# A fused gated convolution, pooling and MLP block on eight cores: staging the output projection's norm chain, issuing MLP weight loads as buffers come free, reordering the first loads and pacing the pooling

## The chip, the cores and the metric

The kernel runs on all 8 cores of one Trainium2 chip. Each core computes 2048 of the 16384 positions by itself; the cores exchange nothing. The metric is device time in microseconds (us) of the slowest core. Some executions fall into a slower state, in which the cores of one die (cores 0 to 3 or 4 to 7) show a lower granted clock (the share of TensorE's full clock that it was allowed, 1.00 at most) and the time is some per cent longer, whatever the kernel. The experiments were made in four groups, each on one chip together with the kernel before, and the chips differ a little: the fast runs of the kernel before lie between 1048.4 and 1053.2 us.

## The reference

```python
u = rms_norm(x, mix_pre_g)
proj = u @ w_in                                   # columns: GLU 2x1024, pooling 1024, gates 2x1024
y_conv = conv_branch(proj[GLU])                   # GLU, depthwise conv 31, layer norm, swish, @ w_conv_out
y_pool = pool_branch(proj[pool])                  # trailing means (2,4,8,16) minus token, per-group linear, @ w_pool_out
merged = sigmoid(g_conv) * y_conv + sigmoid(g_pool) * y_pool
h = x + rms_norm(merged @ w_o, mix_post_g)        # "output projection"
v = rms_norm(h, mlp_pre_g)
v = square(relu(v @ w_ff1)) @ w_ff2               # "FF1", "FF2", hidden width 4096
out = h + rms_norm(v, mlp_post_g)
```

Inputs and outputs are float32, shape (4, 4096, 1024). The kernel multiplies in bf16.

## The kernel before

Every operation goes through a helper that records what it reads and writes and adds the waits, so the order of the calls in Python is the order in which each engine works. That is why most lines of the profile carry the line of a helper: L220 is a matmul, L223 a transpose on TensorE, L238 an ACTIVATE on ScalarE, L241 and L250 are VectorE operations, L262 a weight load issued by POOL that casts float32 to bf16. A load or store on SP's queue is `LOAD` or a plain `dma_start`.

The first loads and the front, in which a tile `x_norm(j)` is normalised, `x_tr(j)` transposes it, and `p_group` multiplies it with the pooling columns of `w_in`:

```python
x_order = [0, 1, 2, 3, -1] + list(range(4, 16))   # -1 is the halo tile of 32 rows
x_load(0); LOAD(grow, gbd[0:1, :]); x_load(1); LOAD(identf, identd); x_load(2); x_load(3); LOAD(vec[:], vecs)
for i in range(2):                                # pooling weights in two pieces
    WLOAD(w_p[:, :, i * 512:(i + 1) * 512], ...)
# ...
for cc in range(4): p_group(cc, 0, 256)
x_tr(2); x_norm(-1); x_tr(3); x_norm(4)
wg_load(0); wg_load(1)                            # 4 MB of GLU weights
for cc in range(4): p_group(cc, 256, 256)
x_tr(-1); x_norm(5)
for cc in range(4, 8):
    p_group(cc, 0, 512)
    if cc == 5 or cc == 6:
        x_tr(cc - 1); x_norm(cc + 1)
p_halo()
for j in (6, 7): x_tr(j); x_norm(j + 2)
# blocks 1 to 3 follow
```

The output projection of a tile of 128 positions, with its two norms in one row of calls:

```python
def resid(b, gb_t, epsc, res, junk, j, eng):
    for hh in range(2): ACT(junk, ps[:, b + hh, :], AF.Square, accum=...)      # sums, ScalarE
    TTE("dve", ...)                                                            # add the halves
    rsqrt(r, ac[0], epsc, eng)                                                 # two operations on POOL
    for hh in range(2):                                                        # scale, add x, VectorE
        STT(ps[:, b + hh, :], ps[:, b + hh, :], r, gb_t[...], ALU.mult, ALU.mult)
        TTE("dve", rs, ps[:, b + hh, :], rs, ALU.add)
    outh[j] = ... dma_start(out=out[128 * j:128 * (j + 1), :], in_=res)        # store h

def wo_tile(j):
    b = banks(2)                                     # 16 matmuls into two PSUM banks
    # ...
    res, dst = xr[j % 3], xb2[j % 2]
    resid(b, gb1, 2, res, dst[:, 0:512], j, "pool")
    r = rstd(res, 128, 0, dst, "pool")               # second norm: ScalarE, then POOL
    STT(dst, res, r, gb2, ALU.mult, ALU.mult)        # VectorE
    if j + 3 < 16: x_reload(j + 3)
```

The four tiles of the last block run between groups of FF1 (block 0), and the weight loads go out of one queue `wq`, one per step:

```python
pend.extend(range(4 * blk, 4 * blk + 4))
for c in (blk, blk + 4): wq.append(lambda c=c: ff1_load(c))
if blk == 3:
    for i in (2, 3, 0, 1): wq.append(lambda i=i: ff2_load(i))
# ...
for i in range(32):
    ff1_group(i, blk)                                # matmuls, relu on VectorE, square on ScalarE
    if blk == 0 and i < 16:
        if i % 4 == 3: wo_step()                     # one wo_tile, one load
        elif i % 4 == 1 and len(trq) > 1: h_tr(trq.popleft())
        if i == 15:
            for s in (4, 5, 6, 7): wq.append(lambda s=s: ff2_load(s))
    if blk == 0 and i >= 16 and wq: wq.popleft()()
```

The FF2 weights lie in eight slots. Slots 4 and 5 hold the residual buffers `xr[0..2]` and a norm gain until the last tile (15) is done, slots 6 and 7 the output weights. FF2 reads the slots in the order 0, 4, 1, 5, 2, 6, 3, 7.

The pooling tasks (VectorE, one for each of 8 channel groups and 4 blocks) are queued and poured out in the first GLU quarter:

```python
for q in range(4):
    for rp in range(8):
        glu_pair(q, rp)
        pump(3)                                      # three pooling tasks
    if q == 0: pump(len(bgd))
```

Of the kernel before, what the change touches and what calls it, by code (L numbers as in the profile page):

```python
# [10 lines left out]
ALU = mybir.AluOpType  # L11
# [159 lines left out]
def build_program():  # L171
# [20 lines left out]
    with ExitStack() as es:  # L192
# [150 lines left out]
        def x_load(j):  # L343
            i = x_order.index(j)
            P, r0 = (32, 0) if j < 0 else (128, H + 128 * j)
            xev[j] = LOAD(xst[i % 4][:P, :], xh[r0:r0 + P, :])

        x_order = [0, 1, 2, 3, -1] + list(range(4, 16))
        x_load(0)
        LOAD(grow, gbd[0:1, :])  # L350
        x_load(1)
        LOAD(identf, identd)
        x_load(2)
        x_load(3)
        LOAD(vec[:], vecs)
        for i in range(2):
            WLOAD(w_p[:, :, i * 512:(i + 1) * 512], w_in_v[:, :, 2048 + i * 512:2048 + (i + 1) * 512])
        for i in range(3):
# [50 lines left out]

        bgd = deque()  # L410

        def pump(n):
# [3 lines left out]

        s2i = {"i": 0}

# [65 lines left out]
        def wg_load(q):  # L484
            for h2 in range(2):
                WLOAD(wg[q % 2][:, :, h2, :], w_in_v[:, :, h2 * 1024 + q * 256:h2 * 1024 + (q + 1) * 256])

        for cc in range(4):
            p_group(cc, 0, 256)
        x_tr(2)  # L490
        x_norm(-1)
        x_tr(3)
        x_norm(4)
        wg_load(0)
        wg_load(1)
        for cc in range(4):
            p_group(cc, 256, 256)
        x_tr(-1)
        x_norm(5)
        for cc in range(4, 8):  # L500
            p_group(cc, 0, 512)
            if cc == 5 or cc == 6:
                x_tr(cc - 1)
                x_norm(cc + 1)
        p_halo()
        for cc in range(8):
            bgd.append(lambda cc=cc: pool_task(cc, 0))
        for j in (6, 7):
            x_tr(j)
            x_norm(j + 2)  # L510
        for blk in range(1, 4):
            for cc in range(8):
                nxt = 4 * (blk + 1) + cc // 2
                if cc % 2 == 0 and nxt + 2 < 16:
                    x_norm(nxt + 2)
                p_group(cc, blk * 512, 512)
                bgd.append(lambda cc=cc, blk=blk: pool_task(cc, blk))
                if cc % 2 == 1 and nxt < 16:
                    x_tr(nxt)
                if cc % 2 == 1 or blk == 3:  # L520
                    pump(1)

# [100 lines left out]
        for q in range(4):  # L623
            glu_halo(q)
            steps = deque(conv_steps(q - 1) if q else [])
            for rp in range(8):
                glu_pair(q, rp)
                pump(3)
                if rp % 2 == 1 and steps:
                    steps.popleft()()  # L630
                if q == 3 and rp % 2 == 0:
                    weff_group(rp // 2)
            if q + 2 < 4:
                wg_load(q + 2)
            if q == 0:
                pump(len(bgd))
            if q == 1:
                weff_prep()
            if q == 2:
                weff_scale()  # L640
                WLOAD(wgp, w_in_v[:, :, 4096:5120])
            if q == 2:
                for r in range(16):
                    bgd.append(lambda r=r: ln_stat(0, r))
# [75 lines left out]

        def resid(b, gb_t, epsc, res, junk, j, eng):
            ac = []
            for hh in range(2):
                a, r = col()
                ACT(junk, ps[:, b + hh, :], AF.Square, scale=1.0 / 32, accum=a)
                ac.append(a)
            TTE("dve", ac[0], ac[0], ac[1], ALU.add)
            r = col()[1]
            rsqrt(r, ac[0], epsc, eng)
            for hh in range(2):  # L730
                rs = res[:, hh * 512:(hh + 1) * 512]
                STT(ps[:, b + hh, :], ps[:, b + hh, :], r, gb_t[:, hh * 512:(hh + 1) * 512], ALU.mult, ALU.mult)
                TTE("dve", rs, ps[:, b + hh, :], rs, ALU.add)
            outh[j] = kb.op("sp", lambda e: e.dma_start(out=out[128 * j:128 * (j + 1), :], in_=res), [res], [("outh", j)], dma=True)

        def x_reload(j):
            LOAD(xr[j % 3], xh[H + 128 * j:H + 128 * (j + 1), :])

        def wo_tile(j):
            b = banks(2)  # L740
            for hh in range(2):
                for k in range(8):
                    MM(ps[:, b + hh, :], m1(j // 4, k)[:, (j % 4) * 128:(j % 4 + 1) * 128], wo[:, k, hh * 512:(hh + 1) * 512], k == 0, k == 7)
            res, dst = xr[j % 3], xb2[j % 2]
            resid(b, gb1, 2, res, dst[:, 0:512], j, "pool")
            r = rstd(res, 128, 0, dst, "pool")
            STT(dst, res, r, gb2, ALU.mult, ALU.mult)
            if j + 3 < 16:
                x_reload(j + 3)

# [16 lines left out]

        def wo_step():

            if pend:  # L770
                j = pend.popleft()
                wo_tile(j)
                trq.append(j)
            if wq:
                wq.popleft()()

        trq = deque()
        wq = deque()
        for blk in range(4):
            for cc in range(8):  # L780
                gated(cc, blk, wco, s_t, wgc, False)
                if blk and cc % 2 == 1:
                    wo_step()
                elif blk and len(trq) > 1:
                    h_tr(trq.popleft())
            pend.extend(range(4 * blk, 4 * blk + 4))
            for c in (blk, blk + 4):
                wq.append(lambda c=c: ff1_load(c))
            if blk == 0:
                wq.popleft()()  # L790
                wq.popleft()()
            if blk == 3:
                for i in (2, 3, 0, 1):
                    wq.append(lambda i=i: ff2_load(i))

# [9 lines left out]
        def ff2_tile(j):  # L805
# [4 lines left out]
            for hh in range(2):  # L810
                for i in range(32):
                    f = FF1_ORDER[i // 4] * 4 + i % 4
                    MM(ps[:, b + hh, :], h1(i)[:, tl * 128:(tl + 1) * 128], ff2(f)[:, hh * 512:(hh + 1) * 512], i == 0, i == 31)
            resid(b, gb3, 0, res, hT[j // 4][:, 0, :], j, "act")

        for blk in range(4):
            for i in range(32):
                ff1_group(i, blk)
                if blk == 0 and i < 16:
                    if i % 4 == 3:  # L820
                        wo_step()
                    elif i % 4 == 1 and len(trq) > 1:
                        h_tr(trq.popleft())
                    if i == 15:
                        for s in (4, 5, 6, 7):
                            wq.append(lambda s=s: ff2_load(s))
                if blk == 0 and i >= 16 and wq:
                    wq.popleft()()
                if blk == 0 and i >= 18 and trq:
                    h_tr(trq.popleft())  # L830
                if blk == 0 and i == 20:
                    LOAD(gb3, gbd[3:4, :].partition_broadcast(128))
            for tl in range(4):
# [77 lines left out]
```

## Time and profile before

| | kernel before |
|---|---|
| fast runs | 1049.79, 1050.14, 1050.25 us |
| slow run | 1194.67 us |
| profiled core (3) | 1048.2 us |
| TensorE busy | 977.5 us |
| idle at 0 to 88 us (front) | 25.7 us |
| idle at 550 to 660 us (FF1, start of FF2) | 30.5 us |

The two idle figures are 88 or 110 us less the busy time of TensorE in the stretches that the prediction shows. The page's first part, busy time of each engine (share of the span) and number of instructions:

```profile
PE 977.5 (93%) x5172; PEld 491.0 (47%) x5172; DVE 424.4 (40%) x688; ACT 312.3 (30%) x570; POOL 60.9 (6%) x110
```

No engine but TensorE is half busy, so time can only be won where TensorE waits. Lines of a timeline give start, length, engine, line, operation, output and input, shapes, the number of instructions in the row and, in brackets, how long the engine had been idle and what ended it.

### The profile page before, as it was taken

The numbers are of one execution on the slowest core, as the hardware profiler recorded it, in microseconds if no ns is written. First come the engines' busy times: TensorE is split into PE (matmuls) and PEld (weight loads), VectorE is DVE, ScalarE is ACT, GpSimd is POOL, SyncE is SP. The second block draws the span as 40 slices with busy tenths as digits, with TensorE's granted clock in tenths as the row PEclk, the third lists the DMA queues.
The fourth block names the chain that finished last, engine by engine and source line by source line (L and its number), as shares of the span: only waits on it lengthen the run. The fifth ranks groups of instructions, "written<-read, shape, count | busy, mean of one in ns | idle before, by whom it ended". The sixth has DMA issues, their size and how long they took to land.

```text
span 1048.2 us, 14416 instructions; the slowest of 8 cores (1043.8 to 1048.2 us)
## 1 busy us (share of the span) xinstructions
PE 977.5 (93%) x5172; PEld 491.0 (47%) x5172; DVE 424.4 (40%) x688; ACT 312.3 (30%) x570; POOL 60.9 (6%) x110
## 2 busy tenths in 40 slices
PE   3799989999999999999998784999999999999996
PEld 2544647766544544444443331444444444444443
DVE  3377843254363123565665440124412342244222
ACT  3663122333213441334333440113311232123211
POOL 2000001000010000112111120000000000000000
PEclk9999989999999999999999998899999999999999
DMA  9925255996990022628484799121001100220021
GB/s 210 200 83 93 50 82 91 146 169 113 163 150 1 1 81 23 138 82 160 115 178 103 129 173 167 42 81 41 1 31 66 65 1 1 81 81 1 1 81 61
DMA packets 47527, 92.53 MB, mean 88 GB/s; under 512 B 6593, under 2 KB 27329, under 8 KB 46306
## 3 DMA queue, kind: packets, MB, share of 16 engines
q0 software_dynamic: 30336, 46.14, 30.5%
q1 hardware_dynamic: 17122, 45.47, 13.2%
q8 instruction: 43, 0.70, 0.3%
q14 instruction: 26, 0.21, 0.1%
HBM read 120.90 MB, written 16.84 MB: 131 GB/s over the span
## 4 chain that ended last, share of the span: by engine, by line
PE 85%; DMA 6%; DVE 4%; issue 2%; ACT 2%; POOL 1%; DVEq 0%; ACTq 0%; POOLq 0%
PE ps L220 82%; DMA arena<-w_ff 4%; PE ps L223 2%; ACT arena L238 2%; DMA arena<-w_in 2%; DVE arena L241 1%; DVE arena L444 1%; DVE ps L246 1%; DVE arena L250 1%; DVE ps L250 0%; POOL arena L262 0%; POOL sm L378 0%; DVEq L159 0%; ACT sm L238 0%; POOL sm L377 0%
## 5 line engine op out<-in xcount | busy, mean ns | idle before, releaser
L220 PE MATMUL ps<-arena 128*128 128x512 bf16 (+4 forms) x4644 | 951.6, 366 | 52.9 <-DMA arena<-w_ff 16.4
L220 PEld LDWEIGHTS ps<-arena 128*128 128x128 bf16 (+2 forms) x4644 | 458.3, 104 | 526.0 <-issue 79.8
L238 ACT ACTIVATE arena<-ps 128x512 bf16<-128x512 f32 (+5 forms) x386 | 237.2, 634 | 624.9 <-PE ps L220 461.1
L246 DVE TENSOR_SCALAR ps<-ps 128x512 f32<-128x512 f32 x128 | 87.3, 697 | 99.9 <-PE ps L220 99.9
L241 DVE TENSOR_TENSOR arena<-ps,arena 128x512 f32<-128x512 f32 (+3 forms) x116 | 86.8, 754 | 88.8 <-ACT arena L238 58.9
L241 DVE TENSOR_TENSOR sm<-sm 128x1 f32<-128x1 f32 x32 | 5.0, 157 | 208.1 <-ACT arena L238 208.1
L250 DVE SCALAR_TENSOR_TENSOR arena<-arena,ps 128x512 bf16<-128x512 f32 (+1 forms) x64 | 43.8, 684 | 99.3 <-ACT arena L238 71.2
L238 ACT ACTIVATE arena<-arena 128x1024 bf16<-128x1024 f32 (+1 forms) x33 | 34.8, 1053 | 91.7 <-DVE arena L241 87.1
L250 DVE SCALAR_TENSOR_TENSOR arena<-arena,sm 128x1024 bf16<-128x1024 f32 (+1 forms) x33 | 42.4, 1284 | 44.0 <-POOL sm L378 41.8
L250 DVE SCALAR_TENSOR_TENSOR ps<-ps,sm,arena 128x512 f32<-128x512 f32 x64 | 48.2, 754 | 21.3 <-POOL sm L378 19.7
L223 PE MATMUL ps<-identb,arena 128*128 128x128 bf16 (+1 forms) x520 | 37.8, 222 | 9.8 <-DVE arena L250 6.3
L223 PEld LDWEIGHTS ps<-identb,arena 128*128 128x128 bf16 (+1 forms) x520 | 33.4, 100 | 21.8 <-issue 12.4
L241 DVE TENSOR_TENSOR arena<-arena 128x512 bf16<-128x512 f32 (+2 forms) x56 | 38.2, 690 | 4.2
L238 ACT ACTIVATE arena<-ps,vec 128x1024 bf16<-128x1024 bf16 x16 | 19.3, 1205 | 2.5 <-PE ps L223 1.7
L586 DVE BATCH_NORM_STATS2 bnst<-arena 128x6 f32<-128x512 bf16 x32 | 20.0, 680 | 0.0
L262 POOL DMA_DIRECT2D arena<-w_ff x16 | 13.7, 863 | 102.2 <-PE ps L220 101.5
L382 DVE RECIPROCAL sm<-sm 128x1 f32<-128x1 f32 (+1 forms) x33 | 5.3, 161 | 35.1 <-ACT sm L238 35.1
L378 POOL TENSOR_TENSOR sm<-sm,mhalf 128x1 f32<-128x1 f32 x32 | 18.1, 567 | 5.0 <-POOL sm L377 0.4
L250 DVE SCALAR_TENSOR_TENSOR arena<-arena 128x512 bf16<-128x512 f32 x24 | 16.5, 687 | 1.6 <-DVE arena L241 0.5
L262 POOL DMA_DIRECT2D arena<-convw x8 | 4.3, 544 | 208.8 <-PE ps L220 136.1
L377 POOL TENSOR_SCALAR sm<-sm 128x1 f32<-128x1 f32 x32 | 7.0, 220 | 155.4 <-DVE sm L241 80.5
L444 DVE TENSOR_TENSOR_SCAN arena<-arena,scr 128x512 f32<-128x512 f32 x12 | 15.4, 1280 | 0.7
(33 smaller groups left out, 82.9 us busy)
## 6 DMA issues: line engine op xcount, KB each, us to landing
arena<-xh SPq DMA_DIRECT2D x32, 512.0 KB, 6.8
arena<-w_ff POOLq DMA_DIRECT2D x16, 1024.0 KB, 16.1
out<-arena SPq DMA_DIRECT2D x32, 512.0 KB, 2.9
arena<-convw POOLq DMA_DIRECT2D x8, 1536.0 KB, 15.4
arena<-out SPq DMA_DIRECT2D x16, 512.0 KB, 4.2
arena<-w_in POOLq DMA_DIRECT2D x8, 512.0 KB, 25.5
arena<-w_in POOLq DMA_DIRECT2D x2, 2048.0 KB, 24.2
arena<-w_in POOLq DMA_DIRECT2D x2, 1024.0 KB, 24.4
```

Of the source, the lines that this page charges most:

```text
L220: kb.op("pe", lambda e: e.matmul(o, lhsT=l, rhs=r, start=start, stop=stop), [l, r], [o])
L223: kb.op("pe", lambda e: e.transpose(o, i, idn), [i, idn], [o])
L238: kb.op("act", lambda e: e.activation(out=o, in_=i, func=func, **kw), rd, wr)
L241: kb.op(eng, lambda e: e.tensor_tensor(out=o, in0=a, in1=b, op=op), [a, b], [o])
L246: kb.op("dve", lambda e: e.tensor_scalar(out=o, in0=a, scalar1=s1, scalar2=s2, op0=op0, **kw), rd, [o])
L250: kb.op("dve", lambda e: e.scalar_tensor_tensor(out=o, in0=a, scalar=s, in1=b, op0=op0, op1=op1), rd, [o])
L262: return kb.op("pool", lambda e: e.dma_start(out=o, in_=src), [], [o], dma=True, after=after)
L377: kb.op("pool", lambda e: e.tensor_scalar(out=o, in0=i, scalar1=EPS[epsc], scalar2=None, op0=ALU.add), [i], [o])
L378: kb.op("pool", lambda e: e.tensor_tensor(out=o, in0=o, in1=mhalf[:, 0:n], op=ALU.pow), [o, mhalf[:, 0:n]], [o])
L382: kb.op("dve", lambda e: e.reciprocal(o, o), [o], [o])
L444: kb.op("dve", lambda e: e.tensor_tensor_scan(so, pc[:, lo:lo + n], pc[:, lo - w:lo - w + n], init, ALU.add, ALU.subtract), rd, [so])
L586: kb.op("dve", lambda e: e.bn_stats(o, i), [i], [o])
```

## The change

Its intent is to take away four waits of TensorE. Pooling tasks come one per GLU pair, over two quarters, in the order in which later buffers overwrite their inputs. The norm chain is cut into stages one slot (two groups) apart, so that VectorE does not stand and wait for ScalarE and POOL inside it. Weight loads of the MLP go out as soon as their buffers are free. And the first loads go out in the order in which they are wanted, in smaller pieces, with the GLU weights moved out of the front.

```diff
-        x_load(0)
-        LOAD(grow, gbd[0:1, :])
-        x_load(1)
+        LOAD(grow, gbd[0:1, :])
+        x_load(0)
         LOAD(identf, identd)
-        x_load(2)
-        x_load(3)
-        LOAD(vec[:], vecs)
-        for i in range(2):
-            WLOAD(w_p[:, :, i * 512:(i + 1) * 512], ...)
+        for j in (1, 2, 3):
+            x_load(j)
+        for i in range(4):                      # x_load(4) waits for the second of these
+            wev.append(WLOAD(w_p[:, :, i * 256:(i + 1) * 256], ...))
 ... (cut)
-        for cc in range(4):
+        for cc in range(2):
             p_group(cc, 0, 256)
         x_tr(2)
         x_norm(-1)
         x_tr(3)
-        x_norm(4)
-        wg_load(0)
-        wg_load(1)
-        for cc in range(4):
+        LOAD(vec[:], vecs)
+        for cc in range(2):
             p_group(cc, 256, 256)
-        x_tr(-1)
-        x_norm(5)
-        for cc in range(4, 8):
+        for cc in range(2, 8):
             p_group(cc, 0, 512)
-            if cc == 5 or cc == 6:
-                x_tr(cc - 1)
-                x_norm(cc + 1)
+            if cc == 3:
+                x_tr(-1)
+                x_norm(4)
+                x_norm(5)
         p_halo()
-        for j in (6, 7):
+        for j in (4, 5, 6, 7):
             x_tr(j)
             x_norm(j + 2)
 ... (cut: wg_load moved into block 1)
                 glu_pair(q, rp)
+                pool_pump(1)
                 pump(3)
-            if q == 0:
-                pump(len(bgd))
             if q == 1:
+                pool_pump(32)
 ... (cut: resid split into resid_a, the sums and the root, and resid_b, the scaling and the store)
+            r = resid_a(b, 2, dst[:, 0:512], "pool")
+            def stage_b():
+                resid_b(b, gb1, r, res, j)
+                v["r"] = rstd(res, 128, 0, dst, "pool")
+            def stage_c():
+                STT(dst, res, v["r"], gb2, ALU.mult, ALU.mult)
+                if j + 3 < 16:
+                    x_reload(j + 3)
+            due.append(deque([stage_b, stage_c, lambda: h_tr(j)]))
+        def tick():                             # one stage of every tile under way
+            for d in list(due):
+                d.popleft()()
 ... (cut)
             pend.extend(range(4 * blk, 4 * blk + 4))
-            for c in (blk, blk + 4):
-                wq.append(lambda c=c: ff1_load(c))
 ... (cut)
+            ff1_load(blk)
+            ff1_load(blk + 4)
+        for i in (2, 3, 0, 1):
+            ff2_load(i)
 ... (cut)
+                if blk == 0 and i % 2 == 1:
+                    tick()
+                    if i % 4 == 3 and pend:
+                        wo_tile(pend.popleft())
+                    if i == 19:
+                        for n in (4, 5, 6, 7):
+                            ff2_load(n)
```

## The prediction

> **What bounds the kernel now.** I read the engine shares first, then busy time by stage, then what the TensorE waits for, then the timeline inside each hole.
>
> ```profile
> PE   3799989999999999999998784999999999999996
> PEclk9999989999999999999999998899999999999999
> ```
>
> Two strips of the page (busy tenths of TensorE, granted clock) in 40 slices of 26.2 us. TensorE is full but for the front and slices 22 to 26. Busy time in stretches, first number after the length being TensorE's:
>
> ```profile
> 0.00:30.00 30.00, 12.96 (x68) 8.00 (x68) 8.11 (x21) 11.02 (x21) 5.62 (x10) 1.00 0.98 205
> 30.00:88.00 58.00, 49.35 (x362) 27.35 (x363) 38.43 (x72) 36.52 (x71) 0.56 (x1) 0.94 0.69 140
> 88.00:148.00 60.00, 55.23 (x250) 31.16 (x249) 45.43 (x67) 12.33 (x21) 2.30 (x3) 0.94 0.42 59
> 440.00:550.00 110.00, 109.51 (x562) 50.69 (x561) 67.40 (x100) 42.78 (x89) 19.57 (x44) 1.00 0.59 134
> 550.00:610.00 60.00, 45.88 (x235) 21.39 (x234) 30.11 (x45) 23.69 (x49) 13.53 (x26) 0.98 0.61 125
> 610.00:660.00 50.00, 33.59 (x131) 13.55 (x130) 8.58 (x13) 10.46 (x18) 1.54 (x3) 0.84 0.95 154
> ```
>
> Idle: 17.0, 8.7, 4.8, 0.5, 14.1, 16.4 us. From 148 to 550 and from 660 on TensorE has no hole worth naming; the last 7.8 us are the tail. The table of waits names the releasers:
>
> ```profile
> PE ps L220 <- DMA arena<-w_ff: 16.4, 4, 6.8
> PE ps L220 <- ACT arena L238: 14.7, 8, 2.9
> PE ps L220 <- DMA arena<-w_in: 6.9, 1, 6.9
> PE ps L220 <- DVE arena L241: 4.8, 1, 4.8
> ```
>
> The 14 us at 550 to 610, one tile of the output projection on the timeline (start, length, engine, idle before):
>
> ```profile
> 573.25 0.76 DVE L250 SCALAR_TENSOR_TENSOR ps<-ps,sm,arena 128x512 f32<-128x512 f32 x1 [1.21 <-POOL sm L378]
> ...
> 578.95 1.28 DVE L250 SCALAR_TENSOR_TENSOR arena<-arena,sm 128x1024 bf16<-128x1024 f32 x1 [2.62 <-POOL sm L378]
> 580.15 2.48 DVE L246 TENSOR_SCALAR ps<-ps 128x512 f32<-128x512 f32 x4
> 580.93 3.58 ACT L238 ACTIVATE arena<-ps 128x512 bf16<-128x512 f32 x6 [3.25 <-DVE ps L246]
> 581.67 3.61 PE L220 MATMUL ps<-arena 128*128 128x512 bf16 x16 [2.63 <-ACT arena L238]
> ```
>
> VectorE stands 1.21 and 2.62 us inside the norm chain waiting for POOL's reciprocal root; four finished FF1 groups wait behind it, no PSUM bank comes free, TensorE stops 2.63 us. The weights hole:
>
> ```profile
> 605.93 2.32 POOL L262 DMA_DIRECT2D arena<-w_ff  x3
> 608.57 2.97 POOL L262 DMA_DIRECT2D arena<-w_ff  x4 [0.32 <-DVE ps L246]
> ...
> 638.42 3.48 PE L220 MATMUL ps<-arena 128*128 128x512 bf16 x8 [6.84 <-DMA arena<-w_ff]
> 644.64 3.16 PE L220 MATMUL ps<-arena 128*128 128x512 bf16 x8 [2.74 <-DMA arena<-w_ff]
> 650.35 1.89 PE L220 MATMUL ps<-arena 128*128 128x512 bf16 x8 [2.55 <-DMA arena<-w_ff]
> 656.53 13.72 PE L220 MATMUL ps<-arena 128*128 128x512 bf16 x50 [4.29 <-DMA arena<-w_ff]
> ```
>
> Seven FF2 weight loads are issued together at 606 to 611 and land one after another, the last four 6.2, 5.7 and 6.2 us apart (mean 6.0). After a hole eight matmuls take 3.48 us where 1.73 is warm (216 ns each, from 16 in 3.46 elsewhere).
>
> **What the Trainium skill says.** (1) "PSUM — Partial Sum Buffer", section "Engine vs sequencer instructions": "ScalarE/VectorE/GpSimdE queues are strict FIFO". The trace agrees: the four evictions at 580.15 start only when the chain's last operation ends. (2) "TensorE: Matmul & The Clock Gate", section "Back-to-back issue gap": N/1.2 ns cold and N/2.4 + 2.5 ns warm, so 427 and 216 at 512 columns; the trace has 435 (3.48/8) after the 6.84 us hole and 216. Holes thus cost more than their length. (3) "DMA: Bandwidth & Descriptors", section "Issuing engines are not separate DMA queues": transfers from all issuers interleave on the same 16 engines. The trace agrees: in 0 to 22 us POOL's queue has 47.6% and SP's 45.7% of the engines.
>
> **The change, part by part.** Matmul work stays the same; only waits can go.
>
> *Pooling paced.* Before, 16 pooling tasks are poured out in the first GLU quarter, three per pair; after, one per pair over two quarters, in the order in which the next buffers overwrite them. A scan task is 1.28 + 0.15 + 0.69 = 2.1 us of VectorE, a pair needs 0.69 more: 2.8 us beside 3.45 us of matmuls (16 x 216 ns), so it keeps up. The second quarter adds the convolution's four evictions of 1.22: 8 x 2.8 + 4.9 = 27 us in about 36. The hole of 4.77 us at 137.9 goes, and with it its cold start (32 matmuls in 9.75 us where 6.9 is warm, 2.85). Gain 7.6 us.
>
> *Norm chain in stages.* After, the sums, then the scaling and residual, then the second norm, then the transposes are issued one slot (two FF1 groups, 3.45 us) apart. The root needs two POOL operations, 0.22 + 0.57, plus hand-over, 1.2 us seen, so it is ready when its reader's turn comes. VectorE has per tile (four FF1 groups) 4 x 0.70 + 0.16 + 2 x (0.75 + 0.69) + 1.28 = 7.1 us in 10.8 us of TensorE (4 x 1.73 + 3.45 + 0.45). The five holes 0.79, 2.93, 2.63, 2.64, 5.14 go: 14.1, plus cold matmuls and transposes after the last (22.85 for 100 where 21.6, and 1.01 where 0.61): 1.7. I leave 0.5 for imperfection: gain 15.3 us.
>
> *FF loads.* FF1 loads and FF2 loads 2, 3, 0, 1 go out at block ends, the last six at about 539 in today's times: 6 x 6.0 = 36 us, all down by 578, long before use. FF2 4 to 7 lie over the residual buffers and the output weights; they stay bound to the last tile's third stage. FF1 begins at 542.2 (counted back from the timeline); 32 groups 55.3, four tiles 13.8, six transposes 2.7 bring FF2's start to 614.0 instead of 630.7. Group 17 ends at 542.2 + 31.1 + 13.8 + 2.3 = 589.3; scaling 0.9 + 2.9, square 1.3, POOL 0.9, final operation 1.3 end at 596.6. Loads issued there land at about 605, 611, 617, 623 (two to start, 6.0 each). FF2 wants slot 4 at 614.9, 5 at 616.6, 6 at 618.3, 7 at 620.1: only slot 7 is late, 3 us, and costs 2 us of cold clock. Before: 16.4 us of waits and cold excess 1.75 + 1.43 + 0.16 + 2.9 = 6.2, sum 22.7. Gain 22.7 - 5 = 17.7 us.
>
> *First loads.* Norm gains and identity come ahead of x1; pooling weights come in four pieces (the first needs half the bytes); 4 MB of GLU weights leave the front. Before, the first projection starts at 21.85, while the transposed x1 was there at 18.3. After, the first piece should be there at 12 (half of 21.5 less the start), so the x chain decides: identity no longer holds the first transpose (cast at 10.6), about 16. Then what is left in: the copy of x3's transpose still stands behind the halo tile's norm on VectorE, so the 4.46 us hole stays; and now all four transposes of x4 to x7 come after the halo, each with its norm (square 1.55, scaling 1.28, copy 1.0 or 0.7 in a row over two engines). I count 7.7 us from halo to block 1, of which 1.8 transposes, against 3.3 before (48.45 to 51.76). Adding up: 16 + 3 + 5.5 + 2.7 + 3.5 + 0.3 + 6.9 + 1.7 + 7.5 = 47.1 against 51.76. Gain 4.7 us, of the 10 that the earlier start suggests.
>
> Sum: 7.6 + 15.3 + 17.7 + 4.7 = 45.3; 1050.25 - 45.3 = 1005 us.
>
> **Rivals.** (a) *The staging makes a PSUM wait.* A tile holds its two banks a slot longer, and in the gated stage the next tile comes to the same pair: its first bank is free 3.8 us after the even group ends (tanh 0.6, two operations 1.4, scaling and add 1.45, hand-overs), wanted at 3.9. It just fits; if late by 1 us, twelve tiles cost 12 us: 1017. For it: that near tie. Against it: banks are released one by one, and that stage has 0.5 us of idle now. (b) *The late FF2 loads stay the bound.* If the third stage slips or four loads share with other traffic, 10 us of wait instead of 3: 1013. (c) *The front gives it all back* (x4's load now waits for the second weight piece): 1010; or it gives 10: 1000. (d) *Denser matmuls pull the granted clock down.* Full stretches show 1.00 now, so I give it little: 2% of the rest would be 1025.
>
> **Range and chances.** Taking (a), (b) or (c) at part strength: 997 to 1017. Two per cent is 21 us; pooling and chain alone give 23, each read from a hole with a known cause. Faster 0.96, same 0.035, slower 0.005.
>
> **What would show it.** Right: no hole at 130 to 138 (in times moved forward); waits on ScalarE near zero during FF1; TensorE's wait on FF weights 2 to 5 us, once; first projection near 16 us and block 1 near 47. Wrong: a wait on VectorE before each tile in the gated stage (a), several waits on FF weights (b), block 1 at 51 or later (c), or matmuls slower than 216 ns in full stretches (d).

## The result, and the profile after

The kernel after ran at 1020.25, 1019.89 and 1021.38 us in fast runs; two runs were slow (1100.13 and 1120.79, with one die at a clock near 0.89). A ratio here is the mean time of one kernel's fast runs over that of the other's of the same rounds, so it is not quite the ratio of the medians quoted. It is 0.9719, with a 95% interval of 0.9696 to 0.9741: faster, by about 30 us. The prediction said 1005 us, with 997 to 1017: the direction is right, and the time lies above the range.

The same two strips of the page as in the prediction, of the kernel after, in 40 slices of 25.5 us:

```profile
PE   4799999999999999999999996999999999999996
PEclk9799999999999999999999997999999999999999
```

Counting slices from 1, the holes of slices 22 to 24 of before are gone and slice 6 is full; one hole is left, in slice 25, at 611 to 636 us, and the front looks much as it did. Busy time in stretches (TensorE's is the first number after the length; the clock stands before the last two numbers):

```profile
0.00:30.00 30.00, 14.76 (x70) 9.16 (x71) 10.22 (x24) 11.94 (x23) 3.88 (x8) 0.91 1.03 196
30.00:88.00 58.00, 49.69 (x346) 25.61 (x344) 30.13 (x50) 34.99 (x67) 4.08 (x5) 0.90 0.73 149
88.00:148.00 60.00, 60.00 (x289) 36.03 (x288) 43.09 (x72) 15.52 (x25) 2.30 (x3) 1.00 0.40 54
...
440.00:550.00 110.00, 108.76 (x554) 50.23 (x552) 68.08 (x101) 45.36 (x93) 24.25 (x50) 1.00 0.66 140
550.00:610.00 60.00, 59.51 (x307) 27.99 (x305) 34.37 (x50) 28.32 (x53) 8.59 (x18) 1.00 1.05 192
610.00:660.00 50.00, 41.09 (x165) 16.94 (x164) 6.26 (x12) 5.43 (x14) 0.00 (x0) 0.86 0.45 94
```

From 88 to 148 TensorE idles 0.0 us instead of 4.8, from 550 to 610 0.5 instead of 14.1. From 610 to 660 it still idles 8.9 us, and the last but one number of the row above says where to look: the DMA engines were full (1.05) in the stretch before. What TensorE waited for:

```profile
PE ps L223 <- DVE arena L250: 10.7, 5, 3.5
PE ps L220 <- DMA arena<-w_ff: 8.9, 3, 3.7
PE ps L220 <- DVE arena L256: 6.3, 2, 4.3
PE ps L220 <- ACT arena L238: 5.4, 4, 1.4
```

ScalarE's 14.7 us became 5.4, of which 4.2 lie before 88 us (three holes of 1.4) and none in FF1. The waits for FF weights fell from 16.4 us in four holes to 8.9 in three. New at the top are 10.7 us of transposes waiting for a normalised tile (L223 for L250) and 6.3 us of projections waiting for a copy (L256): both are the front. This is the timeline of the hole that is left:

```profile
591.19 20.02 PE L220 MATMUL ps<-arena 128*128 128x512 bf16 x92
614.91 3.31 PE L220 MATMUL ps<-arena 128*128 128x512 bf16 x8 [3.71 <-DMA arena<-w_ff]
621.36 2.93 PE L220 MATMUL ps<-arena 128*128 128x512 bf16 x8 [3.14 <-DMA arena<-w_ff]
626.36 24.01 PE L220 MATMUL ps<-arena 128*128 128x512 bf16 x97 [2.07 <-DMA arena<-w_ff]
```

POOL issues the loads. The first row is the six early ones, the second the last four:

```profile
539.82 4.82 POOL L262 DMA_DIRECT2D arena<-w_ff  x6
...
596.54 3.07 POOL L262 DMA_DIRECT2D arena<-w_ff  x4 [7.39 <-DMA out<-arena]
```

POOL stood 7.39 us before the last four, until a store of `out` had read the residual buffer of tile 15. When each load landed is in the trace too:

```
six early loads, issued 539.8 to 543.9, landed  554.7  564.4  572.3  581.9  589.8  600.7
last four loads, issued 596.5 to 598.8, landed  608.4  614.8  621.2  626.2
store of tile 15, issued 586.8, landed 595.8
```

The prediction had the six "all down by 578"; the sixth landed at 600.7. Transfers of the kernel after from 539.8 to 600.8, the time of the six loads, by queue (packets, MB, share of the 16 DMA engines) and by kind (size in KB written, median us from issue to landing):

```profile
q0 software_dynamic: 4282, 6.48, 77.2%
q1 hardware_dynamic: 1428, 5.22, 25.7%
...
arena<-w_ff POOLq DMA_DIRECT2D x10, 1024.0 KB, 25.5
out<-arena SPq DMA_DIRECT2D x5, 512.0 KB, 10.1
arena<-xh SPq DMA_DIRECT2D x2, 512.0 KB, 9.5
```

POOL's queue (q0) and SP's (q1) share full engines. In the kernel before, the last loads fell (619.0 to 656.5 us) in a stretch where POOL's queue had everything to itself:

```profile
q0 software_dynamic: 3082, 6.12, 102.0%
```

From this stretch, 6.12 MB in 37.5 us or 6.1 us a MB, come the 6.0 us per load from which the prediction reckoned; they were FF2 weights alone. An FF1 load that ran alone in the kernel before (578.8 to 590.7 us) was dearer:

```profile
q0 software_dynamic: 1040, 1.05, 72.3%
```

This is 72.3% of 11.9 us, 8.6 us of full engines for one load. And the front of the kernel after, on TensorE:

```profile
16.70 3.57 PE L220 MATMUL ps<-arena 128*128 128x256 bf16 x16 [2.02 <-DVE arena L256]
20.07 1.66 PE L223 MATMUL ps<-identb,arena 128*128 128x128 bf16 x16
26.03 8.05 PE L220 MATMUL ps<-arena 128*128 128x256 bf16 x32 [4.31 <-DVE arena L256]
...
34.31 8.67 PE L220 MATMUL ps<-arena 128*128 128x512 bf16 x96
...
46.57 1.01 PE L223 MATMUL ps<-identb,arena 128*128 128x128 bf16 x8 [2.69 <-DVE arena L250]
49.01 1.01 PE L223 MATMUL ps<-identb,arena 128*128 128x128 bf16 x8 [1.43 <-DVE arena L250]
51.39 5.59 PE L220 MATMUL ps<-arena 128*128 128x512 bf16 x16 [1.37 <-ACT arena L238]
...
87.72 52.47 PE L220 MATMUL ps<-arena 128*128 128x512 bf16 x240 [1.41 <-ACT arena L238]
```

and of the kernel before:

```profile
21.85 6.29 PE L220 MATMUL ps<-arena 128*128 128x256 bf16 x32 [6.86 <-DMA arena<-w_in]
...
33.49 5.32 PE L220 MATMUL ps<-arena 128*128 128x256 bf16 x32 [4.46 <-DVE sm L382]
...
51.76 5.00 PE L220 MATMUL ps<-arena 128*128 128x512 bf16 x16 [1.37 <-ACT arena L238]
...
87.73 45.41 PE L220 MATMUL ps<-arena 128*128 128x512 bf16 x208 [1.65 <-ACT arena L238]
```

The first projection starts 5.2 us earlier, but block 1 starts at 51.39 instead of 51.76 and block 3 at 87.72 instead of 87.73: nothing is left. In between the same work runs slower. A transpose of a tile takes 1.01 us where it takes 0.61 elsewhere, and 16 matmuls of 512 columns take 5.59 where they take 3.61 elsewhere. The trace shows why: the granted clock was 0.50 from 24.8 to 31.4 us and from 45.3 to 55.3 us. Work at this half clock is called cold here, work at 1.00 warm. By the clocks of the first two stretches (0.91 and 0.90 above, 1.00 and 0.94 before) the front spends about 17 us at half clock instead of 7. The lines are those of core 3. In the median of the eight cores the first projection starts at 17.9 us instead of 21.4, and block 1 at 51.7 instead of 50.8.

So the accounts can be read by position. The first tile of the output projection is transposed at 428.75 instead of 435.87: 7.1 us gained, all by the pooling. FF2's last wait ends at 626.36 instead of 656.53: 30.2 us. From there on the two kernels are alike. Of the 45 us that were expected, some 15 are missing: 4.7 in the front and 10 between there and FF2's last wait.

### The profile page after: what moved, and what is told of

It is laid out like the page before. It is cut to its first block, busy times and chain, and to the rows that moved or that the text cites. A ratio compares the mean times of both kernels' runs of the same rounds, so it can differ in the third digit from the quotient of the medians.

```text
span 1018.2 us, 14310 instructions; the slowest of 8 cores (1015.3 to 1018.2 us)
## 1 busy us (share of the span) xinstructions
PE 974.5 (96%) x5156; PEld 489.5 (48%) x5156; DVE 425.1 (42%) x688; ACT 312.6 (31%) x568; POOL 62.4 (6%) x112
## 4 chain that ended last, share of the span: by engine, by line
PE 87%; DMA 4%; DVE 3%; ACT 2%; issue 2%; POOL 0%; DVEq 0%; SPq 0%; ACTq 0%; POOLq 0%
PE ps L220 85%; DMA arena<-w_ff 3%; ACT arena L238 2%; PE ps L223 2%; DVE ps L250 1%; DVE arena L241 1%; DVE arena L250 1%; DMA out<-arena 1%; DMA arena<-xh 1%; POOL arena L262 0%; DVEq L159 0%; DVE arena L256 0%; ACT sm L238 0%; SPq L259 0%; DVE sm L381 0%
## 5 line engine op out<-in xcount | busy, mean ns | idle before, releaser
L220 PE MATMUL ps<-arena 128*128 128x512 bf16 (+3 forms) x4628 | 947.1, 366 | 24.7 <-DMA arena<-w_ff 8.9
L220 PEld LDWEIGHTS ps<-arena 128*128 128x128 bf16 (+1 forms) x4628 | 456.0, 104 | 496.1 <-issue 46.3
L238 ACT ACTIVATE arena<-ps 128x512 bf16<-128x512 f32 (+2 forms) x384 | 238.1, 634 | 627.5 <-PE ps L220 464.2
L241 DVE TENSOR_TENSOR arena<-ps,arena 128x512 f32<-128x512 f32 (+3 forms) x116 | 86.9, 755 | 72.8 <-ACT arena L238 50.1
L250 DVE SCALAR_TENSOR_TENSOR arena<-arena,ps 128x512 bf16<-128x512 f32 (+1 forms) x64 | 44.0, 688 | 142.1 <-ACT arena L238 113.2
L241 DVE TENSOR_TENSOR sm<-sm 128x1 f32<-128x1 f32 x32 | 5.0, 157 | 191.3 <-ACT arena L238 191.3
L223 PE MATMUL ps<-identb,arena 128*128 128x128 bf16 (+1 forms) x520 | 38.7, 226 | 10.9 <-DVE arena L250 10.7
L250 DVE SCALAR_TENSOR_TENSOR ps<-ps,sm,arena 128x512 f32<-128x512 f32 x64 | 48.2, 753 | 1.9 <-DVE sm L381 0.4
L250 DVE SCALAR_TENSOR_TENSOR arena<-arena,sm 128x1024 bf16<-128x1024 f32 (+1 forms) x33 | 42.3, 1282 | 9.2 <-POOL sm L377 7.1
L223 PEld LDWEIGHTS ps<-identb,arena 128*128 128x128 bf16 (+1 forms) x520 | 34.1, 101 | 23.2 <-issue 14.4
L241 DVE TENSOR_TENSOR arena<-arena 128x512 bf16<-128x512 f32 (+2 forms) x56 | 38.5, 691 | 6.5 <-ACT arena L238 2.3
L262 POOL DMA_DIRECT2D arena<-w_in x14 | 12.5, 906 | 108.6 <-DMA arena<-xh 55.5
L250 DVE SCALAR_TENSOR_TENSOR arena<-arena 128x512 bf16<-128x512 f32 x24 | 16.5, 687 | 1.2
L450 DVE TENSOR_TENSOR_SCAN arena<-arena,scr 128x512 f32<-128x512 f32 x12 | 15.3, 1277 | 3.1 <-ACT arena L238 3.1
```

Of the source, the lines that this page charges most:

```text
L220: kb.op("pe", lambda e: e.matmul(o, lhsT=l, rhs=r, start=start, stop=stop), [l, r], [o])
L223: kb.op("pe", lambda e: e.transpose(o, i, idn), [i, idn], [o])
L238: kb.op("act", lambda e: e.activation(out=o, in_=i, func=func, **kw), rd, wr)
L241: kb.op(eng, lambda e: e.tensor_tensor(out=o, in0=a, in1=b, op=op), [a, b], [o])
L250: kb.op("dve", lambda e: e.scalar_tensor_tensor(out=o, in0=a, scalar=s, in1=b, op0=op0, op1=op1), rd, [o])
L262: return kb.op("pool", lambda e: e.dma_start(out=o, in_=src), [], [o], dma=True, after=after)
```

## The experiments

All twelve kernels gave correct results but one. For each missing part there were rival theories. For the loads: either the last four come too late because their issue waits for the store of tile 15, or the loads are a stream at a limited rate and the last ones end late however early they are issued. For the front: the new loads do not matter at all, or the order of the norms on VectorE costs it its gain, or the cold clock does. The expectations name theories by letters, each for itself.

### 1. The front put back (`e1_front_old`)

```diff
 kernel after, with the first loads, wg_load and the order of x_tr, x_norm and p_group as before
```

> The changed kernel with the front of the kernel before (load order, halves of the pooling weights, GLU weights early, groups and transposes in the old order). Theory A (read from the changed kernel's trace: the front gained nothing, because the time it won at 16.7 us was paid back in cold matmuls and in the transposes gathered behind the halo): within 1.5 us of the changed kernel's fast time of 1020 us. Rival B (the prediction: the front gives 4.7 us): 1025 us.

It ran at 1020.10, 1021.56, 1020.20 and 1020.33 us, all fast; ratio 0.9722 (0.9704 to 0.9739), where the kernel after has 0.9719. The whole front part of the change is worth nothing. Its 30 us come from the other three parts.

### 2. Pacing alone (`e2_pool_only`)

```diff
 kernel before
+                pool_pump(1)
                 pump(3)
-            if q == 0:
-                pump(len(bgd))
             if q == 1:
+                pool_pump(32)
 ... (cut: a queue for each channel group, from which the front takes its tasks too)
```

> The kernel before with the pooling order and pacing alone. Prediction and theory A alike: the hole of 4.77 us at 137.9 and its cold start go, 7 to 8 us less than before, 1042.5 us. Rival: the second GLU quarter becomes late on VectorE, so less than 4 us are won.

Four fast runs lie between 1042.32 and 1043.08 us; ratio 0.9931 (0.9915 to 0.9947), so 7.3 us. The 4.77 us hole on `DVE arena L241` is not in its table of waits. This agrees with the 7.6 us predicted and with the 7.1 us read by position.

### 3. Staging alone (`e3_stage_only`)

```diff
 kernel before, with resid_a, resid_b, stage_b, stage_c, tick as in the kernel after; the queue wq stays
+                    if i == 19:
+                        for s in (4, 5, 6, 7): wq.append(lambda s=s: ff2_load(s))
```

The last four loads had to leave the queue two groups later, because they overwrite what the staged chain still reads.

> The kernel before with the norm chain in stages alone; FF loads still one by one from the old queue (the last four put in two groups later, as the new order needs). Theory A: the holes waiting for ScalarE in FF1 go, about 15 us, while the wait on FF weights changes by what the earlier FF1 end brings: TensorE arrives 14 us earlier but the last loads are also issued earlier, so the wait stays at 15 to 25 us: 1033 to 1040 us. Rival B (the loads are the bound whatever the chain does, because their end is fixed by the queue): the wait grows by what the chain gives back, 1046 us or more.

It ran at 1035.22 to 1037.32 us; ratio 0.9869 (0.9854 to 0.9885), so 13.8 us. What TensorE waited for:

```profile
PE ps L220 <- DMA arena<-w_ff: 17.6, 4, 10.3
...
PE ps L220 <- ACT arena L238: 5.7, 4, 1.7
```

ScalarE's 14.7 us fell to 5.7, and none of that lies in FF1, as predicted, and the waits for the weights grew by 1.2 us. The staging is worth nearly what was said, and it does not turn into a wait of its own.

### 4. A separate residual buffer for tile 15 (`e4_res15`)

```diff
 kernel after
+        xr15 = av(TP + 4096, 1024, dt=F32)      # in the place of gb3, which is loaded later
-            LOAD(xr[j % 3], ...)
+            LOAD(xr15 if j == 15 else xr[j % 3], ...)
-            res, dst = xr[j % 3], xb2[j % 2]
+            res, dst = xr15 if j == 15 else xr[j % 3], xb2[j % 2]
```

Tile 15's store no longer reads slot 4, so the last loads need not wait for it.

> The changed kernel with the last tile's residual in a buffer of its own, so that the last four FF2 loads no longer wait for the store of that tile (the trace of the changed kernel shows POOL waiting 7.4 us for it). Theory A (that store, which took 9 to 14 us instead of 2.9 beside six queued weight loads, set the issue of the last four loads): they are issued about 7 us earlier, TensorE waits 8.9 us no more but 0 to 4, time 1009 to 1013 us. Rival C (the rate of the loads is the bound, their issue is not): the wait stays above 7 us and the time within 2 us of 1020.

(The stores beside the early loads took 9.0 to 11.7 us; the 14 was a reload.) It ran at 1022.64, 1024.79, 1025.31 and 1029.43 us (ratio 0.9768, 0.9739 to 0.9797): not faster than the kernel after. The profiled core, 0, had a hole of 6.4 us on a small halo transfer at 225 us, before anything that the edit touches, and its times are some 10.6 us later than those of the kernel after. Cores 2 to 7 of the same profile had no such hole, and they waited for FF weights as well (7.3 to 10.2 us). POOL's timeline and the waits:

```profile
599.85 0.83 POOL L262 DMA_DIRECT2D arena<-w_ff  x1
601.76 2.23 POOL L262 DMA_DIRECT2D arena<-w_ff  x3 [1.08 <-DVE arena L250]
```

```profile
PE ps L220 <- DMA arena<-w_ff: 9.0, 3, 3.8
```

Brought back by 10.6 us, the loads were issued at 589.3 and 591.2 instead of 596.5 and 597.4, 7 and 6 us earlier. The wait is 9.0 us where it was 8.9, and the last load landed at 637.1, or 626.5 in the other kernel's times, where it had landed at 626.2. The theory that the store's wait sets the end falls: the wait was real, but what it held back would not have arrived earlier. The sixth load landed at 598.9 in those times, long after the seventh was issued; the stream itself was still busy.

### 5. Early loads alone (`e5_loads_only`)

```diff
 kernel before
-            for c in (blk, blk + 4):
-                wq.append(lambda c=c: ff1_load(c))
 ... (cut)
+            ff1_load(blk)
+            ff1_load(blk + 4)
+        for i in (2, 3, 0, 1):
+            ff2_load(i)
```

> The kernel before with the FF loads at block ends alone (last four where they were). The previous runs: pooling alone -7.5 us, staging alone -14 us, all three with the old front -30 us, so on top of the others the early loads bring about 9. Theory D (the DMA engines run full from the end of the gated stage to the last load, about 87 us of transfers, whatever TensorE does): with the chain unstaged FF2 starts at 631 us and needs its last load about then, so alone the early loads take away most of the 22.7 us of waiting and cold clock: 1027 to 1033 us. Rival (gains simply add): 9 us, 1041.

Fast runs were 1029.66, 1029.07 and 1028.63 us, against 1048.41 to 1050.22; ratio 0.9809, so 20 us.

```profile
PE ps L220 <- ACT arena L238: 14.4, 8, 2.6
...
PE ps L220 <- DMA arena<-w_ff: 1.4, 1, 1.4
```

With the old chain, the early loads take away nearly all of the 16.4 us of weight waits. Added to a kernel that has the staging and the pacing, the same loads bring some 9 us (30 less 7.3 less 13.8). The gains overlap: the old chain's 14 us of holes in FF1 are 14 us in which the weights travel. Take the holes away and FF2 asks for the weights 14 us earlier.

### 6. The order of the front mended (`e6_front_fix`)

```diff
 kernel after
         x_tr(2)
-        x_norm(-1)
         x_tr(3)
+        x_norm(-1)
 ... (cut, after the block of cc == 3)
+            if cc == 5 or cc == 6:
+                x_tr(cc - 1)
+                x_norm(cc + 1)
-        for j in (4, 5, 6, 7):
+        for j in (6, 7):
```

The copy of tile 3's transpose no longer stands behind the halo's norm, and two of the four transposes lie between groups again.

> The changed kernel; x3's transposes ahead of the halo tile's norm, and the transposes of x4 and x5 between the projection groups again, as before. Theory A (the early start was lost to these two orders and to the cold clock that their holes cause): the hole of 4.3 us shrinks to 1 to 2, that behind the halo from 5.5 to 2; block 1 starts near 44 instead of 51.4; 1013 to 1015 us. Rival (the arrival of x sets block 1, not the order): within 2 us of 1020.

Fast runs were 1010.52, 1012.29 and 1012.86 us; ratio 0.9651 (0.9623 to 0.9679). That is some 7.5 us better than the kernel after. TensorE's timeline (a few matmul records are missing from it):

```profile
23.48 5.36 PE L220 MATMUL ps<-arena 128*128 128x256 bf16 x31 [0.94 <-DVE arena L256]
...
43.20 6.08 PE L220 MATMUL ps<-arena 128*128 128x512 bf16 x15 [1.75 <-DVE arena L250]
```

The hole is 0.94 us where it was 4.31, the 32 projections after it take 5.36 where they took 8.05, and block 1 starts at 43.20, 8.2 us earlier. The earlier loads do have a worth; the order of the work behind them threw it away.

### 7. The same front, kept warm (`e7_warm`)

```diff
 kernel after
+        def warm(n):                             # multiplies the identity by itself, result never read
+            b = banks(1)
+            for _ in range(n):
+                MM(ps[:, b, 0:128], identb[:], identb[:], True, True)
         x_norm(2)
+        warm(24)
         x_tr(1)
         x_norm(3)
+        warm(16)
 ... (cut)
         x_tr(3)
+        warm(50)
 ... (cut, after x_tr of 5, 6, 7)
+            warm(36), warm(18), warm(18)
```

Nothing is moved; TensorE only has something to do in its holes.

> The changed kernel with small matmuls of the identity into a free bank placed in the holes of the front (24, 16, 50, 36, 18, 18 of them); results unchanged. Theory A' (of the 4.3 us by which my count of the front missed, most is cold clock): TensorE stays warm, the 32 projection matmuls after the first hole take about 5.2 us instead of 8.05, the transposes 0.6 instead of 1.0, block 1 starts at 47 to 48.5; 1016 to 1018 us. Rival (the clock plays no part; other engines set the pace): block 1 at 51 and no change in time.

Fast runs were 1015.47 and 1014.37 us (ratio 0.9673, 0.9645 to 0.9701), four others were slow. The profiled run was slow as well, with cores 4 and 5 at a clock of 0.96, so core 1 of the undisturbed die is read (clock 0.994):

```profile
23.94 5.36 PE L220 MATMUL ps<-arena 128*128 128x256 bf16 x32 [1.67 <-DVE arena L256]
...
46.69 3.61 PE L220 MATMUL ps<-arena 128*128 128x512 bf16 x16 [0.37 <-DVE arena L250]
```

With the same order of work as in the kernel after, block 1 starts at 46.69, where the prediction counted 47.1. But core 1 is the earliest: the median of the undisturbed die, cores 0 to 3, is 49.2, against 51.7 on these cores in the kernel after. What the clock costs is better seen in the stretch from the first projection to block 1: 34.6 us in the kernel after, 30.9 kept warm (medians of cores 0 to 3), 31.1 by the count. So some 3.5 us of the miss are cold clock. The rest is the start, which was counted at 16 and came at 17.5 in the median of these cores.

### 8. Two loads left out (`e8_skip2`, wrong on purpose)

```diff
 kernel e4_res15
-        for i in (2, 3, 0, 1):
+        for i in (0, 1):
             ff2_load(i)
```

FF2 then multiplies with what lies in slots 2 and 3, so the result is wrong (relative error 0.54). Against experiment 4, whose edit it contains, it shortens the stream by two loads and changes nothing else.

> As the run with the last residual in its own buffer, but two of the FF2 loads (slots 2 and 3) are never made: the result is wrong on purpose. Theory D (full DMA engines): 2 MB less, each some 6 to 8 us, so the last loads land 13 us earlier and the wait on FF weights falls from 9 us to 0 to 2; about 1007 to 1010 us. Rival (each of the last loads has its own latency after its issue): same wait of about 9 us, since the issue is at the same time.

Fast runs were 1016.84 and 1016.25 us; ratio 0.9689 (0.9661 to 0.9717).

```profile
L262 POOL DMA_DIRECT2D arena<-w_ff x4: 740/756/830, 589.6 to 593.0; - x4
...
  PE ps L220: 7.0, 3
...
DMA to landing us min/median/max: 15.0/23.0/30.1
```

These are durations of the four issues, who waited for them, and how long each load took to land. The last landed at 623.0, only 3.2 us before that of the kernel after and 3.5 before that of experiment 4, where the theory of a plain rate limit had it two loads earlier. The queue was empty before them (the fourth load had landed at 584.1), so here the issue sets the end, which is bound to the last tile's third stage. The four loads took 33.4 us beside a norm gain and a reload. Without these it would be about 29, an estimate: four at 6.0 us, and 5 to start, since a lone FF2 load of the kernel before took 11.0 us from issue to landing (592.4 to 603.4). So there are two floors a few microseconds apart, the stream's pace and the issue after the last tile. An earlier issue alone gained nothing (experiment 4), and with two loads fewer as well the last landing came 3 us earlier.

### 9. The first two FF2 tiles side by side (`e9_ff2_pairs`)

```diff
 kernel after
+        def ff2_pair(j):
+            bs = [banks(2), banks(2)]
+            for half in range(2):                 # slots 0 to 3 for both tiles, then 4 to 7
+                part = [i for i in range(32) if (FF1_ORDER[i // 4] >= 4) == bool(half)]
+                for t in range(2): ...            # matmuls of tile j + t over part
-            for tl in range(4):
+            if blk == 0:
+                ff2_pair(0)
+            for tl in range(2 if blk == 0 else 0, 4):
```

Instead of bringing the weights earlier, this asks for the late ones later: 27.6 us of matmuls over two tiles, of which half need only slots 0 to 3.

> The changed kernel; in FF2 the first two tiles of the first block run together: both halves that need slots 0 to 3 first (64 matmuls, 13.8 us), then both that need slots 4 to 7. Nothing is loaded earlier. Theory D (full DMA engines and a late issue together set the last landing at about 626 us; only using the weights later helps): slot 7 is wanted at about 627, waits on FF weights fall from 8.9 us to 0 to 1 and the 5.8 us of cold matmuls after them go: 1004 to 1008 us. Rival (the loads shift as well, or PSUM of two tiles at once makes new waits): 1012 or more.

Fast runs were 1015.16, 1015.95 and 1016.05 us, against 1050.2 to 1052.0; ratio 0.9665 (0.9644 to 0.9686). It gained 5 us, less than expected; the time is in the rival's range. In the timeline of the profiled core:

```profile
626.49 1.02 PE L220 MATMUL ps<-arena 128*128 128x512 bf16 x4 [0.31 <-DMA arena<-w_ff]
632.01 28.36 PE L220 MATMUL ps<-arena 128*128 128x512 bf16 x118 [4.50 <-DMA arena<-w_ff]
```

One long wait is left. The last load landed at 631.9, 90.0 us after the first of the ten was issued at 541.8; in the kernel after this was 86.4. A second reload of `out`, 512 KB, now lies inside that stretch.

### 10. Mended front and pairs (`e10_combo`)

```diff
 kernel after + e6_front_fix + e9_ff2_pairs
```

> The front with the reordered transposes and FF2 in pairs together. They lie in different stages, so they should add: 7.6 and about 14 us off 1020, 997 to 1001 us. Rival (the earlier arrival at FF2 is eaten by the loads, which end at a fixed distance from the gated stage): 1005 or more.

Fast runs were 1006.41, 1006.20 and 1005.33 us; ratio 0.9569 (0.9552 to 0.9587). The rival held. With the front 8 us earlier the loads began at 531.6 and ended at 624.4, 92.8 us later, and TensorE waited 7.4 us for them: a part of what the front gains is given back here.

### 11. The same, kept warm (`e11_combo_warm`)

```diff
 kernel e10_combo + warm(24), warm(16), warm(12), warm(16), warm(20) in the front
```

> As the combination, with small identity matmuls in the holes of the front that are left (24, 16, 12, 16, 20). If cold clock costs there what the run with warming matmuls showed (16 projection matmuls in 3.6 us instead of 6), 2 to 4 us less than the combination: 994 to 998 us. Rival (the reordered front has too few holes for the clock to matter): within 1 us of the combination.

Fast runs were 1004.33, 1003.31 and 1003.65 us; ratio 0.9548 (0.9531 to 0.9565). The step of 2 us is of the size expected, the level is not: 7.9 us of waits for FF weights are still there.

### 12. Four tiles side by side (`e12_combo_quad`)

```diff
 kernel e11_combo_warm, ff2_pair(0) replaced
+        def ff2_quad(j):
+            bs = [banks(2) for _ in range(4)]     # all eight PSUM banks
+            for half in range(2):
+                for t in range(4): ...            # the residual is reloaded in the second half
```

Half of four tiles is 27.6 us of matmuls before slot 4 is first wanted.

> As the combination with warming matmuls, but all four tiles of FF2's first block do their slot 0 to 3 half first (27.6 us instead of 13.8), so that slot 4 is wanted only about 27 us after FF2 begins. In the pair runs the last load landed 4 to 5 us after it was wanted. Theory D (the DMA stretch from the end of the gated stage to the last landing is fixed at 86 to 93 us by the bytes in it, and only the moment of use can be moved): no wait on FF weights is left (7.9 us in the pair run) nor its cold clock (about 2 us): 992 to 996 us. Rival (the wait moves on, or the four accumulations in all eight PSUM banks make a new wait at their evictions of over 4 us): 999 or more.

Fast runs were 995.20, 995.50 and 998.51 us, against 1049.4 to 1053.2; ratio 0.9479 (0.9452 to 0.9506). It beats both kernels, by 55 us over the kernel before. From the last transpose on there is no hole, and the page's strip shows TensorE full from the third slice to the last but one:

```profile
580.95 149.30 PE L220 MATMUL ps<-arena 128*128 128x512 bf16 x691
```

```profile
PE   6899999999999999999999999999999999999996
```

The last load landed at 620.7, 91.1 us after the first issue: the stream is no faster than before. It is only no longer waited for.

## Why the prediction was right or wrong

**Pooling, 7.6 us predicted.** Right: 7.1 us by position and 7.3 alone (experiment 2).

**Staging, 15.3 us predicted.** Right within 1.5 us: 13.8 alone (experiment 3), and no wait on ScalarE is left in FF1. The rival of a PSUM wait before each tile is nearly absent: a period of the gated stage is 11.1 us after and 11.0 before, which over ten periods is about 1 us.

**FF loads, 17.7 us predicted.** The mechanism was right, and the time of the loads was mis-sized. The step that failed is "6 x 6.0 = 36 us, all down by 578, long before use", and with it "two to start, 6.0 each" for the last four. The 6.0 came from a stretch in which POOL's queue had 102% of the engines and moved FF2 weights alone. In the kernel after, the six loads took 60.9 us from the first issue to the sixth landing. An estimate from the trace covers the 25 us between: SP's queue had 25.7% of these 61 us, 15.7 us; two of the six were FF1 loads, 8.6 instead of 6.1 us each, 5 us; and about 5 to start, as in experiment 8. The last four were issued at 596.5, after the store of tile 15, which took 9.0 us beside the loads: a wait that the prediction left out, though taking it away alone wins nothing (experiment 4). The prediction had 596.6 in the times of the kernel before, and as everything before came 7.1 us earlier, that meant 589.5. The last of them landed at 626.2, where 623 less 7.1 was predicted: 10.3 us too early. Slots 5, 6 and 7 were late, and not slot 7 alone. FF2 then lost 8.9 us of waits, and the cold clock after them another 5.8 (3.31 and 2.93 where 1.73 is warm, and 24.01 for 97 matmuls that take 20.95): 14.8 where 5 had been left, so 9.8 of the missing 15 us. Experiments 4 and 8 show that this has no single cause. The issue after tile 15 and the pace of the stream end within a few microseconds of each other.

**The gains were added up.** Alone, the parts bring 7.3, 13.8 and 20 us, and together 30. The prediction did subtract the staging's 14 us from FF2's start, but with loads that were too fast it saw almost no overlap. Experiment 5 beside the result shows it: 20 us alone, 9 on top of the others.

**Front, 4.7 us predicted.** The mechanism was right again (the work starts earlier). What failed is the sum of the steps behind the start, 47.1: it was 4.3 us too small, nearly all of the gain of 4.7 that was to be left. Set against the timeline: the start at 16.7 instead of 16; 8.0 us instead of 2.7 + 3.5 for the two groups of 256 columns and the next two of 512; 8.6 instead of 7.5 from the halo to block 1 (the prediction's text has 7.7 for it); a microsecond in the smaller terms. The prediction named cold clock after the holes of FF2, but it counted the groups of 512 columns here, 3.5 us for 16 matmuls, as warm. Experiment 7 takes away the cold clock alone and wins back 3.7 us between the first projection and block 1, a stretch that then takes 30.9 us where the count had 31.1 (medians of cores 0 to 3). That core 1 also comes near the predicted 47.1 is luck, for it started early, at 16.7. The rival "the front gives it all back" had named another reason, the later load of tile 4. Experiment 6 moves some norms and transposes, keeps that wait of tile 4's load, and gains 7.5 us, so the wait is not what holds the front back.

**The rivals.** "The late FF2 loads stay the bound" and "the front gives it all back" both came true at about the full strength that the prediction gave them (1013 and 1010, so 8 and 5 us above 1005; measured 9.8 and 4.7). Together they make 1018, and the range had taken one of them at part strength. "Denser matmuls pull the clock down" did not happen: the full stretches show 1.00 before and after.

**The Trainium skill.** The page "TensorE: Matmul & The Clock Gate", section "Why this matters for your kernels", asks for "No PE-idle gaps >~3µs between matmul bursts". The front agrees where it has such a hole: 4.31 us, and 32 matmuls in 8.05 us where 5.36 is warm. Before block 1 each hole is shorter (2.69, 1.43 and 1.37 us), and still the 16 matmuls took 5.59 us instead of 3.61. But only transposes run between these holes: from the end of the last other matmuls, at 43.0, to the next at 51.39 it is 8.4 us. So this does not contradict the page, whose words are "between matmul bursts", if transposes do not count as such; no run tested that alone. The page "DMA: Bandwidth & Descriptors", section "Measured (HBM→SBUF, 128 partitions, SWDGE, issued from GpSimd)", has 6.15 us for 1 MB from a single core and says itself that with both cores of a pair streaming each gets roughly half of what they share. Here an FF2 load writes 1 MB of bf16, cast from 2 MB of float32; one landed every 6.0 us when its core moved nothing else, near the page's time for the bytes written. Beside the other transfers the landings were 9.2 us apart (from 554.7 to 600.7 for five).

**What stays open.** The split of the slower pace into SP's share and dearer FF1 loads is an account of the trace, and no run took one of them away alone. Nor did a run take two loads out of the stream while the store's wait stayed. What the neighbouring cores, which run the same program at the same time, take from a core's pace was not tried either.

## What to carry to other kernels

A load's time must be taken from a stretch with the traffic in which it will run, and two repairs that lie one behind the other (a stall, and weights that travel during that stall) must not be added up: take the first away in thought, then ask again when the second is wanted. When a stream of loads cannot come earlier, reorder the work so that what is wanted early needs only the early loads; this brought 7 us (experiment 12 against 11), where an earlier issue of the loads brought nothing (experiment 4). In a front of short bursts, count the matmuls at the cold rate, or give TensorE something to do in the holes.

## What the Trainium skill lacked or had wrong

- "DMA: Bandwidth & Descriptors" has times for a transfer alone. It says that queues interleave, but has no figure for the pace of two that share full engines: a 512 KB store took 10.1 us (median) beside queued weight loads and 2.9 us (median) over the whole kernel, and weight loads landed 9.2 us apart where 6.0 is the pace alone.
- The same page's table of sizes has no line for loads that cast. A load that casts float32 to bf16 and writes 1.05 MB cost 8.6 us of full engines, 8.2 us a MB, with rows of 512 elements (FF1), and 6.1 us a MB with rows of 1024 (FF2). A lone FF2 load took 11.0 us from issue to landing.
- "TensorE: Matmul & The Clock Gate" tells to warm up for a benchmark, not inside a kernel. Multiplying an identity into a free PSUM bank in the holes of the front brought 5 us in the kernel after (1020.5 to 1014.9, experiment 7) and 2 us where fewer holes were left (experiment 11).
